# A hybrid encoder layer on one core: scan decays from sums sent as rows through DRAM, and the down-projection's weight sums formed one stage earlier

## The chip, the cores and the metric

The kernel runs on one core of a Trainium2 chip. The metric is device microseconds of one execution, the median of the runs shown. Engines are named as in the profile: PE is TensorE (PEld its weight loads), DVE VectorE, ACT ScalarE, POOL GpSimd, SP SyncE, whose instruction stream issues all DMAs here. All data is fp32; products are made from values split into a rounded high part and a rest (`fp32r`), three matmuls for one product (`mm3`: L113, L114, L115).

## The reference

One encoder layer over a prompt of 2048 tokens and a sample of 256 tokens, width 1024: RMSNorm, an input projection, a latent attention group (8 heads) beside a Mamba-2 group (forward and backward scan over chunks of 128 tokens), an output projection, then SwiGLU. What the change touches:

```python
def decay_matrix(a_cs):
    diff = a_cs[..., :, None] - a_cs[..., None, :]
    return jnp.exp(jnp.where(mask, diff, -jnp.inf))       # mask: lower triangle

def ssd_scan(x, dt, a, bmat, cmat):
    xdt = x * dt[..., None]
    a_cs = jnp.cumsum(dt * a, axis=-1)                    # in each chunk
    scores = jnp.einsum('bclhn,bcshn->bchls', cc, bc) * decay_matrix(a_cs)
    y_diag = jnp.einsum('bchls,bcshp->bclhp', scores, xdt)
    ...
def encoder_layer(x, ...):
    ...
    return x + (jax.nn.silu(h @ w_gate) * (h @ w_up)) @ w_down
```

## The kernel before

The 2304 tokens are 18 tiles of 128 (a tile is also a chunk of the scan). The program runs in six stages, one after the other on PE.

**A, projections** (0 to 329 us): q, k, v, z and the scan's dt from the normed input; q, k, v, z and the transposed input (`d_hT`) go to DRAM. The first block is the sample, the next ones are prompt.

**B, SSD** (329 to 745 us): blocks of two tiles. `project` multiplies the x/B/C weights into the next block (96 products of 256 columns a chunk, L113 to L115); the convolution follows on DVE (L469, 16 a chunk) with ACT beside it. `decays(c)` builds the decay matrix of a chunk for both directions: three masked copies on POOL (`rh`, `rl`, `dm`, L488), two matmuls for each half of the heads (L505, L506) that turn the masked step sizes into differences of sums, Exp on ACT (L507), the factor dt on DVE (L508), and the sum of both directions (L510). `turn(c)` transposes the chunk; `scan(c)` multiplies the decays into the scores (L538), forms states (L554, L557, L558) and outputs (L567, L568), and stores `d_y` and `d_sb`. A tile scheduler sets the order on each engine; pools give SBUF slots.

**C, attention** (745 to 1605 us): per head k, v and q are loaded (L654 to L666), scores, softmax and product follow in a written order.

**D, out-projection** (1605 to 1875 us), with the residual stored as `d_x2`.

**E, gate/up** (1883 to 2891 us): a fast (Strassen-like, 7 products for 2x2 blocks) matmul over three groups of six tiles; the operand `hB` is transposed from normed tiles `o` (L919, L932, L933), `U` holds its sums; the weight sums `ws` come from `rawf` loads. SwiGLU's outputs go to DRAM as `d_A`.

**F, down-projection** (2891 us to the end): the same scheme, 7 products by 9 operands by 33 matmuls of 512 columns = 2079 matmuls. `columns(m, j)` (L1114 to L1127) loads blocks of `w_down` (`rawd`), subtracts them on POOL (L1118, L1121, L1124), and splits them on ACT (L1126) and DVE (L1127) into 16 slots `wd`; `operand` loads and splits `d_A` (L1134, L1135).

Of the kernel before, what the change touches and what calls it, by code (L numbers as in the profile page):

```python
# [36 lines left out]
MAGIC = float(0x5F3759DF)  # L37


@with_exitstack  # L40
def hymba_kernel(ctx: ExitStack, tc: tile.TileContext, io, seqs, dbg=None):
# [50 lines left out]
    cmr = const.tile([P, 2, P], F32R, name="cmr")  # L92
    later.append(lambda: nc.vector.tensor_copy(cmr[:, 0, :], m_gt))
    later.append(lambda: nc.vector.tensor_copy(cmr[:, 1, :], m_lt))
# [8 lines left out]
    d_z, d_y, d_C, d_sb = ([dram.tile([P, SW if m != "C" else NG * P], F32, name=f"d_{m}{i}") for i in range(NT)] for m in ("z", "y", "C", "sb"))  # L103
    d_x2 = [dram.tile([P, D], F32, name=f"d_x2{i}") for i in range(NT)]
# [56 lines left out]
    with ExitStack() as ph:  # L161
# [4 lines left out]
        wa = wp.tile([P, 2, KD, WA], F32R, name="wa")  # L166
# [201 lines left out]
    dfs, dtd, dec, dts, dah, dal = (dpool.tile([P, 2, NT, SH], F32, name=m) for m in ("dfs", "dtd", "dec", "dts", "dah", "dal"))  # L368
    dsplit = dpool.tile([P, 2, NT, SH], F32, name="dsplit")

    with ExitStack() as ph:
# [5 lines left out]
        with ExitStack() as inner:  # L377
# [27 lines left out]
            dhr = sb.tile([P, 2, NT, SH], F32R, name="dhr")  # L405
# [3 lines left out]
            nc.vector.tensor_copy(dhr, dsplit)  # L409
            nc.vector.tensor_copy(dah, f(dhr))  # L410
            nc.vector.tensor_tensor(dal, dsplit, dah, op=ALU.subtract)
# [67 lines left out]

        def decays(c, even):  # L480

            w = []
            for d in range(2):
                sign = 1 - 2 * d

                def masked(dst, a):

                    nc.gpsimd.affine_select(dst, a[:, d, c, :].rearrange("p (h o) -> p h o", o=1).to_broadcast([P, SH, P]), pattern=[[0, SH], [sign, P]], compare_op=ALU.is_ge, fill=0.0, base=0, channel_multiplier=-sign)  # L488
# [22 lines left out]
            return w[0]  # L511

# [58 lines left out]
        def decay_sums():  # L571
            for d, (m1, m2) in enumerate(((m_le, m_gt), (m_ge, m_lt))):
# [4 lines left out]
                nc.vector.tensor_tensor(dtd[:, d], dtd[:, d], dts[:, d], op=ALU.mult)  # L577

# [3 lines left out]
        for b in range(nb + 2):  # L582
# [8 lines left out]
            for u in range(4):  # L591
# [21 lines left out]
    mpool = pool(mixer, "mla", 1, side="right")  # L613
# [161 lines left out]

    with ExitStack() as ph:
# [23 lines left out]
        def gather(c):  # L800
# [26 lines left out]
            junk = sb.tile([P, SW], F32, name="junk3", tag="junk3", bufs=1)  # L827
# [7 lines left out]
        def turned(c, y):  # L835
            mT = mp.tile([P, 2, KD, P], F32R, name="mT", tag="mT", bufs=3)
# [7 lines left out]
        def project(c, mT):  # L844
# [9 lines left out]
            if c in order[:4]:  # L854
# [392 lines left out]
```

## Time and profile before

| What | us |
| --- | --- |
| Median of three runs | 3412.65 (3410.53 to 3413.48) |
| The profiled execution | 3416.36 |
| Span of the profile | 3414.7 |
| PE busy | 3244.2 (95% of the span) |
| DVE busy | 2456.1 (72%) |
| ACT busy | 1698.0 (50%) |
| POOL busy | 609.4 (18%) |

A busy time counts instructions in flight; at a lower granted clock the same matmul counts longer. Waits name the instruction that came last before the waiting one could start. The rows of the trace stand in a section of their own below.

### The profile page before, as it was taken

What the parts mean: (1) busy time and instruction counts of PE and PEld (TensorE: products, weight loads), DVE (VectorE), ACT (ScalarE), POOL (GpSimd) and SP (SyncE); (2) the same over time, 40 slices, a digit from 0 to 9 for tenths busy, and PEclk for the clock granted to TensorE, in tenths of its full rate; (3) what the DMA queues carried; (4) which work ended last, traced back from release to release, by engine and by line L of the source; (5) the groups of instructions that cost most, each with busy time, mean ns of one, the idle gap of its engine ahead of it and who ended that gap; (6) DMA issues with size and microseconds to landing.
All of it is one profiled execution on the core that took longest, in us unless ns stands there. A gap on an engine that the chain in (4) does not pass through costs nothing.

```text
span 3414.7 us, 48534 instructions
## 1 busy us (share of the span) xinstructions
PE 3244.2 (95%) x17817; PEld 2882.8 (84%) x17817; DVE 2456.1 (72%) x4396; ACT 1698.0 (50%) x3518; POOL 609.4 (18%) x597
## 2 busy tenths in 40 slices
PE   8998999879999999999799799999999999999988
PEld 7897988858888888887688699999999998778777
DVE  6445799978888888887854777787778776354566
ACT  5453444437777777777311545455544444222233
POOL 2222577750000000000310000000000000432630
PEclk9999999979999999999899899999999999999999
DMA  6565222231022111200642333333333333755664
GB/s 253 191 227 186 90 81 75 69 83 37 27 54 52 39 40 41 54 17 15 224 139 99 142 115 122 142 118 118 137 141 132 113 119 118 230 185 172 224 212 137
DMA packets 259166, 407.24 MB, mean 119 GB/s; under 512 B 21424, under 2 KB 170608, under 8 KB 256368
## 3 DMA queue, kind: packets, MB, share of 16 engines
q1 hardware_dynamic: 258928, 404.15, 35.5%
q8 instruction: 140, 2.29, 0.3%
q14 instruction: 98, 0.80, 0.1%
HBM read 274.98 MB, written 129.11 MB: 118 GB/s over the span
## 4 chain that ended last, share of the span: by engine, by line
PE 78%; DVE 11%; DMA 3%; POOL 3%; issue 3%; ACT 2%; SPq 0%; POOLq 0%; ACTq 0%; DVEq 0%
PE bank_mb L1005 8%; PE bank_ma L1005 8%; PE bank_ta L1005 8%; PE bank_ma L113 6%; PE bank_ma L115 6%; PE bank_ma L114 6%; PE bank_mb L113 5%; PE bank_mb L115 5%; PE bank_mb L114 5%; DVE Y L469 4%; PE bank_ta L721 4%; PE bank_o L729 3%; PE bank_o L730 3%; DMA rawd<-w_down 2%; PE bank_tb L721 2%
## 5 line engine op out<-in xcount | busy, mean ns | idle before, releaser
L938 DVE TENSOR_TENSOR ws<-rawf,ws 128x512 fp32r<-128x512 f32 x396 | 267.8, 687 | 97.2 <-ACT ws L937 95.3
L937 ACT ACTIVATE ws<-rawf 128x512 fp32r<-128x512 f32 x396 | 241.8, 627 | 171.7 <-PE bank_ta L1005 37.2
L1005 PE MATMUL bank_ma<-U,ws 128*128 128x384 f32 x1584 | 302.8, 338 | 6.4 <-ACT U L937 3.2
L1005 PE MATMUL bank_mb<-U,ws 128*128 128x384 f32 x1584 | 304.2, 336 | 2.8 <-ACT c L1014 2.5
L1005 PE MATMUL bank_ta<-U,ws 128*128 128x384 f32 x1584 | 297.3, 334 | 3.5 <-ACT U L937 3.0
L1005 PEld LDWEIGHTS bank_ma<-U,ws 128*128 128x128 f32 x1584 | 279.0, 190 | 8.0 <-ACT U L937 3.5
L129 DVE TENSOR_TENSOR pT<-bank_ta,pT 128x512 fp32r<-128x512 f32 (+1 forms) x352 | 239.6, 681 | 63.2 <-ACT pT L128 54.6
L1005 PEld LDWEIGHTS bank_mb<-U,ws 128*128 128x128 f32 x1584 | 277.4, 189 | 5.1 <-ACT c L1014 4.1
L1005 PEld LDWEIGHTS bank_ta<-U,ws 128*128 128x128 f32 x1584 | 276.7, 188 | 4.5 <-ACT U L937 3.3
L128 ACT ACTIVATE pT<-bank_ta 128x512 fp32r<-128x512 f32 (+1 forms) x352 | 209.1, 595 | 116.7 <-PE bank_ta L721 116.2
L1118 POOL TENSOR_TENSOR rawd<-rawd 128x512 f32<-128x512 f32 x33 | 51.5, 1559 | 1189.0 <-DMA rawd<-w_down 1188.6
L729 PE MATMUL bank_o<-pT,v 128*128 128x512 f32 x528 | 248.7, 471 | 1.9 <-ACT ot L736 1.9
L469 DVE SCALAR_TENSOR_TENSOR Y<-X,cw,Y 128x256 f32<-128x256 f32 x288 | 218.5, 815 | 22.9 <-POOL X L456 15.4
L679 DVE TENSOR_REDUCE mx<-bank_ma 128x1 f32<-128x512 f32 (+1 forms) x261 | 177.0, 678 | 50.1 <-PE bank_ma L115 49.5
L721 PE MATMUL bank_ta<-ident,pr 128*128 128x128 f32 x1388 | 210.6, 273 | 2.0 <-DVE pT L129 2.0
L721 PEld LDWEIGHTS bank_ta<-ident,pr 128*128 128x128 f32 x1388 | 170.5, 140 | 48.7 <-DVE pT L129 8.0
L730 PE MATMUL bank_o<-pT,v 128*128 128x512 f32 x528 | 206.2, 391 | 0.0
L1134 ACT ACTIVATE as<-rawa 128x1408 fp32r<-128x1408 f32 x63 | 86.7, 1378 | 225.6 <-PE bank_ma L115 108.6
L688 ACT ACTIVATE pr<-bank_mb,mx 128x512 f32<-128x512 f32 (+1 forms) x261 | 181.4, 695 | 7.9 <-DVE mx L679 4.8
L688 ACT ACTIVATE pr<-bank_ma,mx 128x512 f32<-128x512 f32 (+1 forms) x261 | 179.1, 686 | 6.4 <-DVE mx L707 5.5
L679 DVE TENSOR_REDUCE mx<-bank_mb 128x1 f32<-128x512 f32 (+1 forms) x261 | 176.9, 678 | 7.0 <-PE bank_mb L115 3.7
L752 POOL TENSOR_TENSOR mla<-lo,ri 128x256 f32<-128x256 f32 (+1 forms) x40 | 22.8, 570 | 855.6 <-DVE lo L751 842.5
(399 smaller groups left out, 8584.9 us busy)
## 6 DMA issues: line engine op xcount, KB each, us to landing
rawf<-w_gu SPq DMA_DIRECT2D x66, 1024.0 KB, 5.8
rawa<-d_A SPq DMA_DIRECT2D x63, 704.0 KB, 5.2
rawd<-w_down SPq DMA_DIRECT2D x154, 256.0 KB, 4.9
d_A<-c SPq DMA_DIRECT2D x132, 192.0 KB, 1.9
d_A<-s SPq DMA_DIRECT2D x99, 192.0 KB, 1.9
o<-d_x SPq DMA_DIRECT2D x32, 512.0 KB, 4.8
d_hT<-hT SPq DMA_DIRECT2D x7, 2048.0 KB, 12.9
hT<-d_hT SPq DMA_DIRECT2D x7, 2048.0 KB, 7.9
```

The costliest lines, as they stand in the source:

```text
L113: nc.tensor.matmul(ps, wh, xh, start=start, stop=False)
L114: nc.tensor.matmul(ps, wh, xl, start=False, stop=False)
L115: nc.tensor.matmul(ps, wl, xh, start=False, stop=stop)
L469: nc.vector.scalar_tensor_tensor(y[:, j, :], x[:, j, t:t + n], cw[:, j, t:t + 1], y[:, j, :], op0=ALU.mult, op1=ALU.add)
L679: nc.vector.tensor_reduce(mx[:, j:j + 1], ps[:, :m * P], axis=AX.X, op=ALU.max, negate=nch == 1)
L688: nc.scalar.activation(e[:, :m * P], ps[:, :m * P], AF.Exp, bias=bias, accum_out=rs[:, i, j:j + 1])
L721: nc.tensor.transpose(ps[:, i * P:(i + 1) * P], pr[i, kt // 4][:, kt % 4 * P:(kt % 4 + 1) * P], ident)
L729: nc.tensor.matmul(po[0][:, :n], v[:, s0 + kt, :], pT[:, 0, :n], start=kt == 0, stop=False)
L730: nc.tensor.matmul(po[0][:, :n], v[:, s0 + kt, :], pT[:, 1, :n], start=False, stop=kt == sn - 1)
L937: nc.scalar.activation(dst[:, 0], src, AF.Copy)
L938: nc.vector.tensor_tensor(dst[:, 1], src, f(dst)[:, 0], op=ALU.subtract)
L1005: nc.tensor.matmul(ps[:, :W], w[:, a, k, :], x[:, b, k, :], start=k + n == 0 and not more, stop=k == HK - 1 and n == 2, skip_group_check=more)
```

## The change

It has five parts.

1. **Decays as rows.** Sums over a chunk are formed once (`decay_sums`: a coarse and a fine part of the steps, each multiplied by the triangle, and ln dt less the fine sum), transposed and stored to DRAM by `cum_rows` (`d_cum`, `d_off`). For each chunk `load_rows` brings them back by 14 small DMAs (6 of 32 KB, 8 of 4 KB) into `rows0/1` and `offs0/1`; `decays` multiplies these, adds a large negative mask by a second matmul (`never`, `identr`), and Exp gives decay times dt. The masked copies (L488) and the factor dt (L508) go. `d_cum` has to be zero off its diagonal: one DMA of 3.98 MB copies zeros into it at the start. The conv's edge copies (L455, L456) go from POOL to ACT.
2. **Sums of weight blocks in gate/up.** In the third group of stage E, `sums(j)` loads two row blocks of `w_down`, makes four subtractions on POOL and stores the results as `d_B`; stage F loads these, so the subtractions in `columns` go.
3. **Early columns and operands in F.** Five columns of the next product and one operand are prepared ahead; `as` takes the slots of `hB`; the residual's addition (L1176) goes from POOL to DVE.
4. **The first gate/up operand in D.** `columns_of(0, 0)` transposes the first three tiles inside the out-projection; the pools of E stand in another order.
5. **Alignment.** `wa` is padded from 432 to 448 columns, `f_pad` shifts `wd`, and the attention's pool `mla` goes to the other side of SBUF.

```diff
+            if b == 1:
+                nc.sync.dma_start(d_cum.rearrange("q g x -> (q g) x"), io["c_zero"])
...
-                rh = mp.tile([P, SH, P], F32R, name="rh", tag="rh")
-                rl = sb.tile([P, SH, P], F32R, name="rl", tag="rl", bufs=1)
-                dm = sb.tile([P, SH, P], F32, name="dm", tag="dm", bufs=1)
-                masked(rh, dah)
-                masked(rl, dal)
-                masked(dm, dts)
+                r, o = fix[d]
...
-                    nc.tensor.matmul(pd, cmr[:, d, :], rh[:, s, :], start=True, stop=False)
-                    nc.tensor.matmul(pd, cmr[:, d, :], rl[:, s, :], start=False, stop=True)
+                    nc.tensor.matmul(pd, o, r[:, s, :], start=True, stop=False)
+                    nc.tensor.matmul(pd, identr, never[:, d:d + 1, :].to_broadcast([P, 4, P]), start=False, stop=True)
                     nc.scalar.activation(e[:, s, :], pd, AF.Exp)
-                nc.vector.tensor_tensor(e, e, dm, op=ALU.mult)
...
+        def load_rows(c):
+            for d in range(2):
+                r, o = fix[d]
+                for q in range(3):
+                    at = (0, 8, 32)[q]
+                    nc.sync.dma_start(f(r)[at:at + SH], d_cum[q, d * NT + c, :SH * SH * P].rearrange("(h x l) -> h x l", h=SH, l=P))
+                for q in range(4):
+                    at = (16, 24, 40, 48)[q]
+                    nc.sync.dma_start(f(o)[at:at + SH], d_off[q, d * NT + c])
...
+        def cum_rows():
+
+            d_diag = d_cum.rearrange("q (t r) (h x) -> q (r h) t x", t=3, h=SH)[..., :P]
+            for src, qc, qo in ((coarse, (0, 1), (0, 1)), (fine, (2,), ()), (off, (), (2, 3))):
...
                     decay[c] = decays(c, b % 2 == 0)
+                    if c + 1 < NT:
+                        load_rows(c + 1)
...
-    mpool = pool(mixer, "mla", 1, side="right")
+    mpool = pool(mixer, "mla", 1)
...
+            if c == order[G]:
+                columns_of(0, 0, [first_xs.pop(t) for t in order[:G]])
...
+        def sums(j):
+
+            top, low = (op.tile([P, D], F32, name="o", tag="o") for _ in range(2))
+            nc.gpsimd.tensor_copy(top[:, :1], C["c11", 0][:, :1])
+            nc.sync.dma_start(top, io["w_down"][j])
+            nc.sync.dma_start(low, io["w_down"][j + HF])
+            b11, b12, b21, b22 = top[:, :512], top[:, 512:], low[:, :512], low[:, 512:]
+            for m, out, x, y in ((5, b11, b12, b11), (7, b12, b22, b12), (6, b22, b22, b11), (4, b21, b21, b22)):
+                nc.gpsimd.tensor_tensor(out, x, y, op=ALU.subtract)
+                nc.sync.dma_start(d_B[m][:, j], out)
...
-        rp = pool(ph, "f_raw", 6)
+        rp = pool(ph, "f_raw", 4)
...
+                nc.sync.dma_start(raw, d_B[m][:, j])
...
+        prepare(1, AHEAD)
+        ahead = operand(*work[0])
+        for i, (m, s, t) in enumerate(work):
+            lo, hi = parts[s]
+            prepare(m, HF)
+            a = ahead
+            if i + 1 < len(work):
+                ahead = operand(*work[i + 1])
+            if i % n_m == n_m - 2 and i + 2 < len(work):
+                prepare(work[i + 2][0], AHEAD)
```

**SP at the start of stage A**, before: `cs` is a table, `xt` the input, `raw` the weights of z, kv and q, `d_hT` a store.

```order
L207 DMA cs<-c_rope 128x32 x2
L184 DMA xt<-x 128x1024 x4
L207 DMA cs<-c_rope 128x32
L174 DMA raw<-w_z 128x1024 x3
L174 DMA raw<-w_kv 128x1024
L174 DMA raw<-w_q 128x2x384 x2
L338 DMA d_hT_84<-hT 128x4096
```

Now:

```order
L209 DMA cs<-c_rope 128x32 x2
L186 DMA xt<-x 128x1024 x4
L209 DMA cs<-c_rope 128x32
L329 DMA d_cum<-c_zero 64x15552
L176 DMA raw<-w_z 128x1024 x3
L176 DMA raw<-w_kv 128x1024
L176 DMA raw<-w_q 128x2x384
L342 DMA d_hT_83<-hT 128x4096
```

The copy of zeros `d_cum<-c_zero` stands ahead of the three loads of z's weights and all that follows them.

**SP in the scan's loop**, before: `hT` is the next block's input, `d_C`, `d_y` and `d_sb` are the chunks' stores.

```order
L427 DMA hT<-d_hT_84 128x4096
L569 DMA d_y_126<-yo 128x512
L473 DMA d_C_145<-Y 256x1x128
L473 DMA d_C_146<-Y 256x1x128
L564 DMA d_sb_162<-ns_6111 128x512
L569 DMA d_y_127<-yo 128x512
L564 DMA d_sb_163<-ns_6345 128x512
```

Now (`rows`, `offs`: what `load_rows` brings):

```order
L433 DMA hT<-d_hT_83 128x4096
L508 DMA rows_3521<-d_cum 8x1024 x3
L511 DMA offs_3522<-d_off 8x128 x2
L608 DMA d_y_125<-yo 128x512
L511 DMA offs_3522<-d_off 8x128 x2
L479 DMA d_C_144<-Y 256x1x128
L479 DMA d_C_145<-Y 256x1x128
L508 DMA rows_3527<-d_cum 8x1024 x3
L511 DMA offs_3528<-d_off 8x128 x4
L603 DMA d_sb_161<-ns_6185 128x512
L508 DMA rows_3521<-d_cum 8x1024 x2
L608 DMA d_y_126<-yo 128x512
```

Fourteen loads a chunk now stand between the stores, those of one direction in a row.

**SP at the end of the scan**, before: `k` and `v` are those of attention's first head.

```order
L564 DMA d_sb_165<-ns_6789 128x512
L654 DMA k<-d_k_93 64x4608
L655 DMA k<-d_kr 32x4608
L657 DMA v<-d_v 128x18x128
L569 DMA d_y_130<-yo 128x512
L564 DMA d_sb_166<-ns_6999 128x512
L473 DMA d_C_151<-Y 256x1x128
L473 DMA d_C_152<-Y 256x1x128
```

Now:

```order
L603 DMA d_sb_166<-ns_7156 128x512
L608 DMA d_y_131<-yo 128x512
L608 DMA d_y_132<-yo 128x512
L603 DMA d_sb_167<-ns_7239 128x512
L603 DMA d_sb_168<-ns_7301 128x512
L608 DMA d_y_133<-yo 128x512
L603 DMA d_sb_169<-ns_7351 128x512
L702 DMA k<-d_k_92 64x4608
L703 DMA k<-d_kr 32x4608
```

The first head's `k` and `v` were issued among the stores of the chunks, five chunks ahead of the last; they now stand behind the last `d_sb`.

## Rows read from the trace of the kernel before

**Rows 1.** Busy time by stage; columns: stretch, its length, engines, granted clock, DMA

```profile
329.00:745.00 416.00, 362.58 (x2467) 335.17 (x2468) 364.03 (x414) 168.26 (x264) 292.51 (x268) 0.92 0.22 75
745.00:1605.00 860.00, 847.71 (x4759) 691.79 (x4759) 705.86 (x1276) 662.09 (x1647) 21.18 (x37) 0.99 0.16 41
...
1900.00:2891.00 991.00, 979.25 (x5638) 972.66 (x5638) 748.20 (x1355) 475.42 (x889) 0.00 (x0) 0.99 0.34 122
```

**Rows 2.** The same view: the scan's loop and its tail

```profile
345.00:685.00 340.00, 309.64 (x2232) 292.04 (x2231) 301.68 (x352) 146.64 (x231) 239.80 (x226) 0.96 0.24 81
685.00:745.00 60.00, 41.68 (x170) 32.99 (x169) 48.63 (x51) 15.09 (x23) 41.77 (x30) 0.72 0.12 43
```

**Rows 3.** Groups of VectorE, 329 to 745 us; columns: busy, mean, idle and releaser

```profile
L469 DVE SCALAR_TENSOR_TENSOR Y<-X,cw,Y 128x256 f32<-128x256 f32 x288 | 218.5, 815 | 22.9 <-POOL X L456 15.4 <-ACT Y L467 7.2
L508 DVE TENSOR_TENSOR e<-e,dm 128x1024 f32<-128x1024 f32 x36 | 60.9, 1691 | 14.5 <-ACT e L507 6.5 <-POOL dm L488 4.3 <-POOL rh L488 3.7
```

**Rows 4.** The convolution's line L469 by itself

```profile
L469 DVE SCALAR_TENSOR_TENSOR Y<-X,cw,Y x288: 468/476/1511, 334.4 to 710.4; 128x256 f32<-128x256 f32 x144
```

**Rows 5.** Groups of GpSimd, 329 to 745 us

```profile
L488 POOL TENSOR_SCALAR_AFFINE_SELECT rh<-dah 128x1024 fp32r<-128x1024 f32 x36 | 52.9, 1470 | 38.7 <-PE bank_ta L505 38.7
L488 POOL TENSOR_SCALAR_AFFINE_SELECT rl<-dal 128x1024 fp32r<-128x1024 f32 x36 | 51.3, 1424 | 0.0
...
L488 POOL TENSOR_SCALAR_AFFINE_SELECT dm<-dts 128x1024 f32<-128x1024 f32 x36 | 47.5, 1320 | 31.4 <-DVE e L508 31.4
```

**Rows 6.** Waits of TensorE, whole span; columns: total us, times, longest us

```profile
PE bank_o L567 <- DVE e L538: 23.3, 12, 3.5
PE bank_tb L554 <- DVE ns L558: 21.3, 9, 5.9
...
PE bank_ma L113 <- ACT as L1134: 10.0, 3, 6.6
...
PE bank_mb L113 <- ACT wd L1126: 7.4, 3, 4.6
```

**Rows 7.** Timeline of SyncE around the scan's end; columns: start, length

```profile
671.53 0.52 SPq L654 DMA_DIRECT2D k<-d_k  x1
...
747.30 0.32 SPq L564 DMA_DIRECT2D d_sb<-ns  x1
```

**Rows 8.** DMA issues: KB each, median us from issue to landing

```profile
d_hT<-hT SPq DMA_DIRECT2D x7, 2048.0 KB, 12.9
hT<-d_hT SPq DMA_DIRECT2D x7, 2048.0 KB, 7.9
...
k<-d_k SPq DMA_DIRECT2D x8, 1152.0 KB, 9.3
...
d_y<-yo SPq DMA_DIRECT2D x18, 256.0 KB, 2.0
```

**Rows 9.** Timeline of SyncE at the start

```profile
16.64 2.56 SPq L174 DMA_DIRECT2D raw<-w_z  x3
```

**Rows 10.** Timeline of TensorE, out-projection to gate/up

```profile
1874.55 0.39 PE L115 MATMUL bank_mb<-wo,mT 128*128 128x512 f32 x1
...
1883.45 1.01 PE L1005 MATMUL bank_ma<-U,ws 128*128 128x384 f32 x2 [1.76 <-ACT ws L937]
...
1899.98 0.48 PE L932 MATMUL bank_tb<-ident,o 128*128 128x128 f32 x1 [9.15 <-DVE o L919]
```

**Rows 11.** Busy time in three stretches of the down-projection

```profile
2891.00:2997.00 106.00, 91.97 (x378) 73.70 (x377) 48.23 (x45) 36.95 (x48) 44.71 (x29) 0.92 0.77 238
3100.00:3200.00 100.00, 100.00 (x442) 82.81 (x442) 53.31 (x56) 29.44 (x33) 29.52 (x14) 1.00 0.59 183
3220.00:3300.00 80.00, 65.51 (x259) 50.95 (x258) 45.02 (x63) 20.73 (x26) 57.14 (x30) 0.91 0.75 241
```

**Rows 12.** Groups of the down-projection

```profile
L1118 POOL TENSOR_TENSOR rawd<-rawd 128x512 f32<-128x512 f32 x33 | 51.5, 1559 | 1189.0 <-DMA rawd<-w_down 1188.6
L1126 ACT ACTIVATE wd<-rawd 128x512 fp32r<-128x512 f32 x76 | 44.3, 623 | 98.9 <-POOL rawd L1124 57.6 <-POOL rawd L1121 19.3 <-POOL rawd L1114 11.3
```

More of the change, by code (lines that the diff above doesn't have):

```diff
@@ L367, in hymba_kernel @@
     dpool = pool(mixer, "decays", 1)
-    dfs, dtd, dec, dts, dah, dal = (dpool.tile([P, 2, NT, SH], F32, name=m) for m in ("dfs", "dtd", "dec", "dts", "dah", "dal"))
+    dfs, dtd, dec, dts, coarse, fine, off = (dpool.tile([P, 2, NT, SH], F32, name=m) for m in ("dfs", "dtd", "dec", "dts", "coarse", "fine", "off"))
     dsplit = dpool.tile([P, 2, NT, SH], F32, name="dsplit")
@@ L511, in decays @@
             return w[0]
+        def cum_rows():
+            d_diag = d_cum.rearrange("q (t r) (h x) -> q (r h) t x", t=3, h=SH)[..., :P]
+            for src, qc, qo in ((coarse, (0, 1), (0, 1)), (fine, (2,), ()), (off, (), (2, 3))):
+                flat = src.rearrange("p d c h -> p (d c h)")
+                ps = bank("mb")[:96, :384]
+                for t in range(3):
+                    nc.tensor.transpose(ps[:, t * P:(t + 1) * P], flat[:, t * 96:(t + 1) * 96], ident)
+                part = sb.tile([96, 2, 3, P], F32R, name="part", tag="Y")
+                flatp = part.rearrange("p q t l -> p q (t l)")
+                nc.scalar.activation(flatp[:, 0], ps, AF.Copy)
+                if src is not fine:
+                    nc.vector.tensor_tensor(flatp[:, 1], ps, f(flatp)[:, 0], op=ALU.subtract)
+                for i, q in enumerate(qc):
+                    nc.sync.dma_start(d_diag[q], f(part)[:, i])
+                for i, q in enumerate(qo):
+                    nc.sync.dma_start(d_off[q].rearrange("(t r) h l -> (r h) t l", t=3), f(part)[:, i])
         def turn(c, y):
@@ L577, in decay_sums @@
                 nc.vector.tensor_tensor(dtd[:, d], dtd[:, d], dts[:, d], op=ALU.mult)
+                for t in (coarse, fine):
+                    ps = bank("mb")[:, :NT * SH]
+                    nc.tensor.matmul(ps, m1, t[:, d].rearrange("p c h -> p (c h)"), start=True, stop=True)
+                    nc.vector.tensor_copy(t[:, d], ps.rearrange("p (c h) -> p c h", h=SH))
+                nc.vector.tensor_tensor(off[:, d], off[:, d], fine[:, d], op=ALU.subtract)
+            cum_rows()
+            load_rows(bl[0][0])
         nb = len(bl)
@@ L773, in hymba_kernel, with columns_of @@
                 step()
+    G = 3
+    W = G * P
+    assert NT % (2 * G) == 0
+    order = [c for c, _ in falling(1)]
+    parts = [(order[i:i + G], order[i + G:i + 2 * G]) for i in range(0, NT, 2 * G)]
+    hbs = [pool(ctx, "e_hb0", 1, side="right")]
+    H, first_xs = {}, {}
+    def columns_of(s, half, xs):
+        h = hbs[half].tile([P, KD, W], F32, name=f"hB{half}", tag="hB")
+        for k in range(KD):
+            ps = bank(("tb", "o")[k % 2])
+            for i in range(G):
+                nc.tensor.transpose(ps[:, i * P:(i + 1) * P], xs[i][:, k * P:(k + 1) * P], ident)
+            nc.scalar.activation(h[:, k, :], ps[:, :W], AF.Copy, scale=g_ffn[:, k:k + 1])
+        H[s, half] = h
     with ExitStack() as ph:
@@ L1081, in hymba_kernel @@
                 weights(*groups[i + AHEAD])
+            if s + 1 == len(parts) and u and m == 1:
+                sums(j)
             if s + 1 < len(parts) and u:
@@ L1224, in layout @@
     ang = np.arange(s, dtype=np.float32)[:, None] * inv[None, :]
+    rk = np.zeros((P, P + SH * P), np.float32)
+    rk[:16, :P] = rk[32:40, :P] = 1.0
+    for q, at in enumerate((16, 24, 40, 48)):
+        rk[at:at + SH, P:] = np.repeat(np.eye(SH), P, axis=1) * (1.0 if q > 1 else -1.0)
+    out["c_rk"] = rk
+    out["c_zero"] = np.zeros((6 * (a["x_prompt"].shape[1] + a["x_sample"].shape[1]) // P, SH * (SH + 1) * P), np.float32)
     out["c_rope"] = np.stack([np.cos(ang), np.sin(ang)], axis=1).astype(np.float32)
```

171 lines of the change are left out of this document (81 added, 90 removed).

## The prediction

> **What bounds the kernel now.** I read the busy times by stage first, then cut the stages whose sum is short of their length, then the waits, then the groups and the timelines at those places. PE is busy for 3244.2 of 3414.7 us, so at most 170 us are idle; but a matmul counts longer at a low clock, so the idle hides more. Attention and gate/up leave little: 847.7 of 860 and 979.3 of 991 us, at a clock of 0.99 [rows 1]. The SSD stage leaves most: 362.6 of 416, with DVE at 364.0, POOL at 292.5 [rows 1]. Inside it there are two regimes. In the loop PE is busy for 309.6 of 340 us at a clock of 0.96, DVE for 301.7; in the tail, where no projection is left to fill gaps, PE for 41.7 of 60 at 0.72 [rows 2]. PE's two longest waits of the whole program lie here, L567 for e of L538 (23.3 us) and L554 for ns of L558 (21.3 us), both for DVE [rows 6]. DVE is slow there for a reason: L469 takes 476 ns as a median and 815 as a mean [rows 3, 4], the rest being stretch while POOL runs its masked copies [rows 5]. The second place is the down-projection. 442 matmuls fill 100 us undisturbed, so one takes 0.2262; but 378 take 106 us at its start, 259 take 80 us at 3220 [rows 11]. Those stretches wait for operands and columns (L1134, L1126) [rows 6], and the columns wait for POOL [rows 12]. The third is the seam into gate/up: the last out-projection matmul starts at 1874.55, the first product at 1883.45, and a transpose at 1899.98 has waited for 9.15 us [rows 10].
>
> **The change part by part.** The sum is made against the profiled execution, 3416.36 us, which lies 3.7 above the median.
>
> *Zeros at the start.* One copy of 3.98 MB goes ahead of z's weights, issued at 16.64 now [rows 9]. The nearest rows: a load of 2 MB lands after 7.9 us, a store of 2 MB after 12.9 as a median [rows 8]. So the copy holds the queue for 16 (two loads) to 26 us (two stores), or for as little as 10 if it moves at twice the load's rate. The order of PE is changed too: z's matmuls of the sample stand behind other work. I take +5, with 0 and +15 as ends, since the queue may also let the weights overtake. The Trainium skill, "DMA: Bandwidth & Descriptors", section "Latency and other measured facts", gives 207 to 214 GB/s for copies between HBM tensors; from this an estimate of 19 us for the copy, inside these ends, and no row here shows such a copy.
>
> *The scan's loop.* Gone from POOL are three groups of 36 copies, 52.9 + 51.3 + 47.5 = 151.7 us [rows 5], and small edge copies; some 115 of 292.5 us stay. Gone from DVE are 36 products L508, 60.9 us [rows 3]. L469's stretch is 288 x (0.815 - 0.476) = 97.6 us [rows 3, 4]; if it scales with POOL's time, 115/292.5, 38 us of it are left, so 59 more go. DVE falls from 364 to about 364 - 61 - 59 = 244 us, a third less. Added are no PE instructions: two matmuls of 512 columns take the place of two. Then PE sets the pace: 309.6 us at a clock of 0.96 are 297 at full clock, and with some 8 us of gaps left the loop takes 305 instead of 340, **-35**; I take -32, with -15 (only half of the waits of rows 6 go) and -43 (no gap at all) as ends. This term rests on the row loads being hidden. They are 14 a chunk, and a chunk takes 340/18 = 19 us or more; DMAs of 256 KB land after 2.0 us [rows 8], and issues follow each other by 0.5 us (0.52 for k) [rows 7], so 14 x 0.5 + 2 = 9 us if they overlap. Behind them in SP's order stand the stores d_y, d_sb, d_C and the load of hT, none of which PE needs within a chunk. If a load of hT (7.9 us) is in front, 17 us: still hidden, though barely.
>
> The rule that speaks against this: in the Trainium skill, the page "DMA: Bandwidth & Descriptors", section "Rules for kernel authors", says that many small transfers should be made one, since under 64 KB one pays mostly overhead. All 14 are under 64 KB. By the rule the overhead is paid on the queue, and as long as it is under a chunk's time the sum stays; where it isn't is the third rival.
>
> *The scan's start.* Sums, nine transposes, seven stores to DRAM and the first 14 loads stand in a chain ahead of the first decays: 2.0 for a store, 2.0 + 7 for the loads, an estimated 3 for three copies of about an ACT group's length [rows 12] between, 12 to 14 us; beside it the first blocks' projections run, and the waits for rh go. +3, with -2 and +10 as ends.
>
> *The tail.* 60 us, in which DVE is busy for 48.6 [rows 2]. By the same third, 32 us of DVE; PE needs 41.7 x 0.72 = 30 us at full clock. The chain through both is serial in part: a third off its 60 us gives 40, and 3 more for loads that a shorter chunk covers less: 43, **-17**, ends -8 and -24. What is late next is the rows: here chunks follow faster than in the loop, and 9 us of loads stand in each.
>
> *Attention's first loads.* The first head's k is issued at 671.53, 74 us ahead of the last d_sb at 747.30 [rows 7], and lands long before it is wanted. In the changed order it stands behind the last d_sb. A k load takes 9.3 us [rows 8], v behind it a little longer; PE has nothing else to do, and goes cold. **+11**, ends +5 (short because the tail's last work covers some) and +15.
>
> *Attention and alignment.* The matmul counts don't change. Addresses do, in attention and in the down-projection. 512 columns at 2.4 GHz are 213.3 ns, an undisturbed one takes 226.2 [rows 11]; no row shows the same matmul at another address, so what of the 12.9 ns between is due to the address is unknown. I take 0, the value for an address without effect, with a loss or a gain as ends; rival (4) has the gain's price.
>
> *The seam into gate/up.* From 1874.55 to the transpose at 1899.98 are 25 us, in which 9.15 + some 5 us PE idles and the clock is low [rows 10]. The first operand is now ready in D; its U sums still wait for DVE and ACT. **-10**, ends -4 and -15. The transposes are moved, not removed.
>
> *Sums in gate/up.* 44 subtractions of 1.56 us [rows 12] are 69 us of POOL in the last third, 330 us, where POOL does nothing now; at L469's price, 97.6/292.5 = 0.33 us of DVE for one of POOL, that is 23 us on a DVE that is busy for 748 of 991 [rows 1]. Hidden by DVE's room; and 66 DMAs more, behind which the rawf loads stand on SP. +2, ends 0 and +8.
>
> *The down-projection.* The two disturbed stretches lose 106 - 378 x 0.2262 = 20.5 and 80 - 259 x 0.2262 = 21.4 us [rows 11], together 42. POOL leaves the columns' path, five columns and one operand are there early, each column is one load instead of up to four. What remains is some 6 us at the stage's start. **-36**, ends -22 and -42.
>
> Sum: 5 - 32 + 3 - 17 + 11 + 0 - 10 + 2 - 36 = **-74**: 3416.4 - 74 = 3342 profiled, 3339 as a median.
>
> **The rivals.**
> (1) *Half of the scan.* The waits for DVE go, and waits for rows or for the chain ns to L554 come, so that the loop gives -15 and the tail -8: 26 us less, 3365. For it: the scan's state is a chain through PE, POOL (L557) and DVE, which the change doesn't shorten. Against: most waits of rows 6 name DVE while it is full.
> (2) *The down-projection keeps half.* Five early columns of eleven are not enough, or four rawd buffers instead of six bind, 3357 to 3360; with (1) 3383.
> (3) *Slower: the rows bind.* If the 14 loads went one behind the other, each landing before the next, they would take 14 x 2.0 = 28 us a chunk [rows 8], and 18 chunks 504 us, 160 more than the forecast has: 3500. The change is slower than before from 74/18 = 4.1 us a chunk beyond 19, that is from 1.65 us for a load. For it: one queue, in order, and tiles with one buffer each, so a chunk's rows can't come before the last chunk's are read. Against: three loads of z's weights, each twice the 256 KB that take 2.0 us [rows 8], are issued within 2.56 us [rows 9], so one doesn't wait for the landing of the last.
> (4) *Alignment counts.* If the shifted operands save all of the 12.9 ns in each of the down-projection's 2079 matmuls, that is 27 us: 3312, and lower if attention's do too. The rows speak neither for it nor against it; by the same token a matmul could become slower.
> (5) *The zeros stall PE.* If z's weights wait for the whole copy at the store's rate and PE finds nothing else, that is 26 us instead of 5: 3360.
>
> **How the numbers follow.** Forecast (3325 to 3355) 0.50; (1) 0.15; (2) 0.08; (4) 0.09; (5) 0.08; (3) 0.07; gains and costs that cancel to no difference 0.03. The likeliest is 3339. The range goes from 3300, which takes in (4) with a few us of attention's, to 3390, which takes in (5), (1), (2) and (2) with (1); what is out is (3), no difference, and the far end of (4): about 0.14. Under 0.2% (6.8 us) can't be told from no change; faster by more 0.90, within 0.03, slower 0.07.
>
> **What would show it.** In the scan: L469's mean near 0.6 us, L508 gone, PE's loop at 300 to 310 us with a clock near 1; a wait of the L505 matmuls for DMA rows would show (1) or (3). After the last d_sb, PE waiting for some 10 us for a DMA of k. At 17 to 50 us, PE waiting for z's weights for under 15 us. In the down-projection, 2079 matmuls in 476 to 482 us and no wait for wd of more than 3 us; rows of rawd waiting for a buffer would show (2). The forecast is wrong if the loop stays over 325 us, or if the copy of zeros stalls PE for 20.

## The result, and the profile after

The changed kernel takes 3352.47 us as a median (3351.20 to 3356.65, four runs) against 3411.86 of before (3410.53 to 3413.48): the ratio is 0.9825, with a 95% interval of 0.9814 to 0.9837, or 59 us faster. The forecast was 3339, its range 3300 to 3390. The profiled execution has a span of 3350.0 us against 3414.7, 64.7 less.

The stages are cut here at the starts of the same matmuls in the two traces, and each term of the prediction stands beside its stretch. The second row holds the prediction's loop and the scan's start before it. Attention's first product is that of the softmax with v (L729 before, L777 after); the first scores, k with q, come ahead of it. The first block of gate/up is its first 168 matmuls.

| Stretch | Before | After | Change | Predicted |
| --- | --- | --- | --- | --- |
| Start to the first scan projection | 305.8 | 308.8 | +3.0 | +5 (zeros) |
| First to last scan projection | 371.2 | 327.3 | -43.9 | -32 and +3 |
| To the last L593 (L554 before) | 69.0 | 52.5 | -16.5 | -17 |
| To attention's first product | 25.9 | 41.4 | +15.5 | +11 |
| Attention and out-projection | 1102.7 | 1102.2 | -0.5 | 0 |
| Seam and first block of gate/up | 68.6 | 48.1 | -20.5 | -10 |
| Rest of the first two groups | 626.6 | 626.6 | 0.0 | |
| Third group of gate/up | 321.2 | 344.3 | +23.1 | +2 |
| Down-projection | 514.1 | 489.3 | -24.8 | -36 |
| End | 9.6 | 9.5 | -0.1 | |

The sum, -64.7, is 9 short of the forecast -74, but four terms are off by ten or more, two each way. The busy times of the scan after (columns as in [rows 2]), first the loop, then the tail:

```profile
348.00:636.00 288.00, 287.69 (x2195) 278.15 (x2195) 208.59 (x323) 146.88 (x276) 84.98 (x79) 1.00 0.28 97
636.00:689.00 53.00, 41.20 (x204) 32.90 (x202) 35.70 (x52) 21.30 (x36) 25.49 (x19) 0.86 0.22 71
```

PE has no gap left in the loop, 287.69 of 288 us at a clock of 1.00, where [rows 2] show 0.96; DVE has come down to 209 us of 288. DVE's convolution there:

```profile
L475 DVE SCALAR_TENSOR_TENSOR Y<-X,cw,Y 128x256 f32<-128x256 f32 x288 | 172.4, 660 | 31.8 <-ACT X L462 30.9 <-ACT Y L473 0.9
```

```profile
L475 DVE SCALAR_TENSOR_TENSOR Y<-X,cw,Y x288: 464/476/1518, 348.3 to 664.0; 128x256 f32<-128x256 f32 x144
```

The mean fell from 815 to 660 ns, the median is 476 as in [rows 4]. TensorE's waits after, of the whole span:

```profile
PE bank_ta L1071 <- DVE c L1085: 13.9, 9, 4.0
PE bank_ma L115 <- DMA k<-d_kr: 12.9, 1, 12.9
...
PE bank_ma L115 <- ACT as L1194: 4.6, 1, 4.6
PE bank_tb L593 <- DVE ns L597: 4.2, 2, 3.3
...
PE bank_o L606 <- DVE e L577: 3.1, 2, 2.5
```

The 23.3 and 21.3 us of [rows 6] for the scan are now 3.1 for e and 4.2 for ns. Two waits are new: 12.9 us for the first head's k and 13.9 us in nine pieces for DVE's L1085 in gate/up. The timeline of SP shows where the first comes from, and that of PE where it ends:

```profile
689.88 0.32 SPq L603 DMA_DIRECT2D d_sb<-ns  x1
690.30 0.52 SPq L702 DMA_DIRECT2D k<-d_k  x1
```

```profile
687.45 1.72 PE L593 MATMUL bank_tb<-xd,bt 128*128 128x256 f32 x4 [0.95 <-DVE ns L597]
702.10 0.77 PE L115 MATMUL bank_ma<-k,q 96*128 96x512 f32 x1 [12.93 <-DMA k<-d_kr]
702.67 0.63 PE L116 MATMUL bank_ma<-k,q 96*128 96x512 f32 x1
703.09 0.63 PE L117 MATMUL bank_ma<-k,q 96*128 96x512 f32 x1
```

The load of k stands right behind the last `d_sb`, as the order said, and the first score starts 12 us later; the matmuls behind it follow each other at 0.42 us, where [rows 11] have 0.226 at full clock. Before, k was issued at 671.53 [rows 7], and 18 of the first head's score matmuls ran inside the scan's tail, from 683.95 on; now all of them come behind it. The zeros show at the start on POOL, which splits z's weights. Before, and then after:

```profile
24.54 1.06 POOL L119 TENSOR_SCALAR wz<-raw 128x1024 fp32r<-128x1024 f32 x1 [10.15 <-DMA raw<-w_z]
```

```profile
38.19 3.04 POOL L121 TENSOR_SCALAR wz<-raw 128x1024 fp32r<-128x1024 f32 x2 [5.42 <-DMA raw<-w_z]
```

The weights come 13.7 us later on POOL, but PE, with z's products moved behind other work, loses 3.0 of them. The DMA records of the trace show the copy itself: its 64 rows of 62,208 bytes move between 21.0 and 33.5 us, that is 3.98 MB in 12.4 us, and end 16.7 us after the issue at 16.76.

### The profile page after: what moved, and what is told of

Its sections match the earlier page's. It is cut to its first block, busy times and chain, and to the rows that moved or that the text cites. A ratio compares the mean times of both kernels' runs of the same rounds, so it can differ in the third digit from the quotient of the medians.

```text
span 3350.0 us, 48726 instructions
## 1 busy us (share of the span) xinstructions
PE 3220.2 (96%) x17834; PEld 2869.8 (86%) x17834; DVE 2347.6 (70%) x4390; ACT 1703.3 (51%) x3576; POOL 344.9 (10%) x393
## 4 chain that ended last, share of the span: by engine, by line
PE 80%; DVE 8%; DMA 6%; ACT 2%; issue 2%; POOL 2%; SPq 0%; ACTq 0%; DVEq 0%; POOLq 0%
PE bank_ma L115 8%; PE bank_ma L117 8%; PE bank_ma L116 8%; PE bank_ma L1071 6%; PE bank_mb L1071 6%; PE bank_ta L1071 6%; PE bank_mb L115 6%; PE bank_mb L117 6%; PE bank_mb L116 6%; PE bank_ta L769 4%; PE bank_o L777 3%; PE bank_o L778 3%; PE bank_tb L769 2%; DMA rawf<-w_gu 1%; DVE ws L1004 1%
## 5 line engine op out<-in xcount | busy, mean ns | idle before, releaser
L1004 DVE TENSOR_TENSOR ws<-rawf,ws 128x512 fp32r<-128x512 f32 x396 | 278.6, 717 | 68.8 <-ACT ws L1003 67.6
L1071 PE MATMUL bank_ta<-U,ws 128*128 128x384 f32 x1584 | 301.6, 337 | 21.2 <-DVE c L1085 13.9
L777 PE MATMUL bank_o<-pT,v 128*128 128x512 f32 x528 | 249.7, 473 | 1.9 <-ACT ot L784 1.9
L475 DVE SCALAR_TENSOR_TENSOR Y<-X,cw,Y 128x256 f32<-128x256 f32 x288 | 172.4, 660 | 31.8 <-ACT X L462 30.9
L736 ACT ACTIVATE pr<-bank_ma,mx 128x512 f32<-128x512 f32 (+1 forms) x261 | 179.1, 686 | 20.5 <-DVE mx L755 19.4
L117 PE MATMUL bank_ma<-hT,wx 128*128 128x256 f32 x576 | 164.7, 286 | 2.7 <-DVE wx L126 2.7
L115 PE MATMUL bank_ma<-hT,wx 128*128 128x256 f32 x576 | 166.9, 290 | 0.3 <-ACT wx L123 0.3
```

What stands on the lines that cost most here:

```text
L115: nc.tensor.matmul(ps, wh, xh, start=start, stop=False)
L117: nc.tensor.matmul(ps, wl, xh, start=False, stop=stop)
L736: nc.scalar.activation(e[:, :m * P], ps[:, :m * P], AF.Exp, bias=bias, accum_out=rs[:, i, j:j + 1])
L777: nc.tensor.matmul(po[0][:, :n], v[:, s0 + kt, :], pT[:, 0, :n], start=kt == 0, stop=False)
L1004: nc.vector.tensor_tensor(dst[:, 1], src, f(dst)[:, 0], op=ALU.subtract)
L1071: nc.tensor.matmul(ps[:, :W], w[:, a, k, :], x[:, b, k, :], start=k + n == 0 and not more, stop=k == HK - 1 and n == 2, skip_group_check=more)
```

## The experiments

A time without a range behind it is a single run. Stretches that the kernels leave alone differ a little among the traces: the third group of gate/up takes 342.3 to 347.1 us in six kernels that share it, the down-projection 488.3 to 491.9 in eight. A difference of that size shows nothing.

**The scan alone.** The kernel before with part 1 of the change and nothing else; attention's pool stays on the right side, so that k keeps its place. The line is shown against the changed kernel, and parts 2 to 5 are missing too.

```diff
-    mpool = pool(mixer, "mla", 1)
+    mpool = pool(mixer, "mla", 1, side="right")
```

> The kernel before with the decays as rows alone (zeros, sums, rows, the conv's edge copies on ACT), attention's pool where it was; here the first k keeps its place ahead of the last stores. Theory, from the two traces: start +3, loop -44, tail -16, and no wait for k: -57 or 3355. Rival: the 15 us at the seam are due to the rows' own end, not to k's slots: 3370.

Measured: 3355.11 us (3354.25 to 3356.35), ratio 0.9832 (0.9817 to 0.9846). The loop is 327.0, the tail 51.3 and the stretch to the first product 27.1 us, not 41.4. So the scan gives 58 us, and all the rest of the change together 2.6 (4.6 by the spans of the profiles), which the two intervals do not tell from nothing. That rest is made of gains and losses: against this kernel the seam gains 69.2 - 48.1 = 21.1 and the down-projection 510.7 - 489.3 = 21.4, and of these 42.5 go 41.4 - 27.1 = 14.3 to k and 344.3 - 321.2 = 23.1 to the weight sums.

**k early.**

```diff
+        kvs = [pool(ph, "c_kv0", 1)]
+        qp = pool(ph, "c_q", 2)
         lp = pool(ph, "c_l", 2)
-        qp = pool(ph, "c_q", 2)
-        kvs = [pool(ph, "c_kv0", 1)]
```

> The changed kernel with the attention's pools opened in another order (k and v of even heads first, then q, then the rest), so that the first head's k and v get the slots of the projection weights, which are free from 636 us on, and stand five chunks ahead of the last d_sb in SP's order. Theory: the wait of the first scores for k (12.9 us) and the cold stretch behind it are what the change pays at this seam, 15.0 us between the last L593 and the last out-projection matmul; the time falls by 13 to 16 us, to 3336 to 3340. Rival: the first scores can't do much before the first head's softmax has filled its pipeline, so the wait moves to the row maxima; the time falls by 3 at most, to 3349.

Measured: 3340.13 us (3338.37 to 3340.77), 12.3 under the changed kernel; the stretch to attention's first product is 27.0 us, as in the scan alone. PE behind the last L593:

```profile
690.02 0.50 PE L115 MATMUL bank_tb<-k,q 96*128 96x512 f32 x1 [0.74 <-ACT ns L599]
...
693.75 0.79 PE L115 MATMUL bank_ma<-k,q 96*128 96x512 f32 x1 [2.76 <-ACT pr L736]
```

The first scores run inside the scan's tail again (18 matmuls, from 649.6 us on), and the next ones follow the scan at once; 2.8 us of the rival's wait for the softmax are left. The theory's mechanism holds; its gain falls 0.7 us short of the range.

**The weight sums in attention.**

```diff
+                if nch > 1 and h > 1 and todo_sums:
+                    sums(todo_sums.popleft(), ri[:, 0, :])
...
-            if s + 1 == len(parts) and u and m == 1:
-                sums(j)
```

> The changed kernel with the weight-block sums (loads, four subtractions on POOL, stores) moved from the third group of gate/up into the attention, eleven times after a block of 512 rows. Theory: POOL's subtractions slow those DVE instructions that read both inputs from SBUF, and gate/up has them while attention's read one from PSUM; the third group goes from 344 back to 321 us, attention stays at 829, F's start gains 0 to 4: 3326 to 3331. Rival: DVE in attention (busy for 706 of 860 us) is slowed as much, and the gain comes back there: 3340 or more.

Measured: 3330.52 us (3329.47 to 3332.08), 22.0 under the changed kernel. The third group is 321.7 us; attention, from its first product to its last score, is 829.2 in both; the down-projection is 488.6: its start gained nothing. So the rival fell. DVE's groups in the third group show why the place matters. In the changed kernel, with POOL's subtractions beside them:

```profile
L1004 DVE TENSOR_TENSOR ws<-rawf,ws 128x512 fp32r<-128x512 f32 x126 | 95.7, 781 | 4.7 <-ACT ws L1003 4.7
L1089 DVE TENSOR_TENSOR c<-c,c 128x384 f32<-128x384 f32 x32 | 25.9, 810 | 1.0
L1085 DVE TENSOR_TENSOR c<-bank_ta,c 128x384 f32<-128x384 f32 x42 | 23.1, 550 | 4.6 <-PE bank_ta L1071 4.4
```

And with the sums in attention:

```profile
L1008 DVE TENSOR_TENSOR ws<-rawf,ws 128x512 fp32r<-128x512 f32 x137 | 92.2, 688 | 39.1 <-ACT ws L1007 38.8
L1089 DVE TENSOR_TENSOR c<-bank_ta,c 128x384 f32<-128x384 f32 x44 | 24.2, 551 | 2.1 <-ACT c L1084 1.2 <-PE bank_ta L1075 0.9
L1093 DVE TENSOR_TENSOR c<-c,c 128x384 f32<-128x384 f32 x34 | 18.8, 553 | 1.0
```

The split of `ws` is 781 ns against 688 and the sum `c<-c,c` 810 against 553, both with two inputs in SBUF; `c<-bank_ta,c`, with one of them in PSUM, is 550 against 551. The Trainium skill, "SBUF — State Buffer", says under "Who interferes with whom" that a VectorE instruction with two SBUF inputs contends with a GpSimd instruction that reads SBUF, and one with at most one SBUF input, outside the 2-port modes, does not; these three rows agree. In attention the largest group of DVE, with one input in PSUM (`pT<-bank_ta,pT`), takes 689 ns with the sums and without.

But it is not this stretch that PE waits for in most of the group. The changed kernel's trace shows another way, by the order of SP, here once in full:

```profile
2674.73 4.88 POOL L999 TENSOR_TENSOR o<-o 128x512 f32<-128x512 f32 x3 [0.95 <-DMA d_A<-c]
```

```profile
2679.64 0.32 SPq L1000 DMA_DIRECT2D d_B<-o  x1
2680.05 2.15 SPq L1039 DMA_DIRECT2D rawf<-w_gu  x2
```

```profile
2686.39 0.69 DVE L1049 TENSOR_TENSOR S<-rawf 128x512 f32<-128x512 f32 x1 [9.28 <-DMA rawf<-w_gu]
```

```profile
2689.41 2.38 PE L1071 MATMUL bank_ta<-U,ws 128*128 128x384 f32 x12 [2.20 <-DVE c L1085]
```

A store of `d_B` waits until POOL has made its block; the load of the next weights, `rawf`, is issued behind it; DVE sits idle for 9.28 us until that load lands, and L1085, for which PE waits, comes 2.4 us later. Eight of the nine waits for L1085 come 3.0 us after the end of such a wait of DVE, 10.0 us in all; the ninth, 3.95, stands at the group's end, behind DVE's split of the early operand (`as`). DVE's waits for `rawf` in the third group, in the changed kernel and then with the sums in attention:

```profile
DVE S L1049 <- DMA rawf<-w_gu: 69.1, 10, 9.3
```

```profile
DVE S L1053 <- DMA rawf<-w_gu: 28.3, 10, 3.2
```

Only at the group's start does PE wait beside stretched instructions with no such load in front: 4.3 us for DVE's `U`, while POOL makes its first four blocks.

**The traffic without the subtractions.**

```diff
-                nc.gpsimd.tensor_tensor(out, x, y, op=ALU.subtract)
```

> The changed kernel without the four subtractions on POOL in the third group of gate/up; the loads and the stores stay, so that raw blocks are stored as sums and the down-projection multiplies wrong weights (this part of the computation is left out). Theory (POOL's reads hold up DVE's instructions with two SBUF inputs): the third group goes from 344 to 321 to 324 us, the whole to about 3329. Rival (66 more DMAs and stores in SP's order hold the gate/up loads back): it stays at 338 or more, the whole at 3346 or more.

Measured: 3332.63 us; the third group takes 324.9. So POOL's subtractions cost 19.4 of the 23.1 us, and the 66 DMAs, with POOL's one-column copies that stay, 3.7, which is hardly more than the traces differ by. The theory's number holds, but the run does not tell its reason from the other: without the subtractions the stores don't wait for POOL either, and DVE's waits for `rawf` are 28.2 us.

**Shorter subtractions.**

```diff
-                nc.gpsimd.tensor_tensor(out, x, y, op=ALU.subtract)
+                for p in range(0, 512, 128):
+                    nc.gpsimd.tensor_tensor(out[:, p:p + 128], x[:, p:p + 128], y[:, p:p + 128], op=ALU.subtract)
```

> The changed kernel with each of the 44 subtractions cut into four of 128 columns. The same work on POOL in shorter instructions. Theory: DVE waits for the POOL instruction that is in flight, 1.56 us at most now and some 0.4 to 0.5 then, and PE waits only where a DVE instruction is late by more than its bank's slack; the third group falls to 325 to 333 us. Rival: what counts is POOL's time in sum, which grows with the fixed time of 132 more instructions; the third group stays at 344 or rises to 350.

Measured: 3365.27 us, the third group 358.3, slower by 14. POOL's group in the changed kernel, then in this one, and this one's largest wait of PE there, a group of DVE and SP's waits for POOL:

```profile
L999 POOL TENSOR_TENSOR o<-o 128x512 f32<-128x512 f32 x44 | 70.6, 1604 | 56.8 <-DMA o<-w_down 51.1 <-DMA d_A<-c 3.8
```

```profile
L1000 POOL TENSOR_TENSOR o<-o 128x128 f32<-128x128 f32 x176 | 105.4, 637 | 47.9 <-DMA o<-w_down 47.9
```

```profile
PE bank_ta L1072 <- DVE c L1086: 21.8, 11, 4.1
```

```profile
L1090 DVE TENSOR_TENSOR c<-c,c 128x384 f32<-128x384 f32 x32 | 18.9, 590 | 1.0
```

```profile
SPq L1001 <- POOL o L1000: 80.6, 44, 3.7
```

The theory, that the single wait matters, fell; the group even rose above the rival's 350. POOL's time rose from 70.6 to 105.4 us, and less the 3.7 of the DMAs PE lost 19.4 and 33.4: 0.27 and 0.32 us for each us of POOL. DVE is stretched less (`c<-c,c` 590 ns instead of 810; DVE is busy for 243 us of the group instead of 255, and for 235 without the subtractions), and PE loses more. So the stretch is not what PE pays for. SP's waits for POOL fit: 80.6 us instead of 56.0, and with them DVE's waits for `rawf`, 85.4 instead of 69.1. No run changes SP's order alone.

**The subtractions on DVE.**

```diff
-                nc.gpsimd.tensor_tensor(out, x, y, op=ALU.subtract)
+                nc.vector.tensor_tensor(out, x, y, op=ALU.subtract)
```

> The changed kernel with the 44 subtractions on DVE instead of POOL. DVE gets 44 x 0.69 = 30 us more in a stretch of 330 us where it is busy for 241, and POOL is idle. Theory: no instruction is stretched, the third group is 321 to 325 us, the whole 3329 to 3333. Rival: DVE's queue is in order, a subtraction waits for its load, and what stands behind it waits too: 335 or more.

Measured: 3345.16 us (3343.36 to 3347.32), the third group 337.0: 7 less than on POOL, 12 more than with the traffic alone, 15 more than with the sums in attention. The subtractions in DVE's queue, and PE's waits:

```profile
L999 DVE TENSOR_TENSOR o<-o 128x512 f32<-128x512 f32 x44 | 30.2, 686 | 25.8 <-DMA o<-w_down 25.5
```

```profile
PE bank_ta L1071 <- DVE c L1085: 6.7, 2, 6.4
PE bank_ta L1071 <- DVE ws L1004: 4.1, 4, 1.5
```

The theory's first half holds: with POOL idle the splits of `ws` and the sums `c<-c,c` take 682 and 549 ns, so no instruction is stretched. The subtractions take 0.69 us each, 30.2 in all, as expected, but DVE sits idle for 25.5 us until their loads land, SP waits for DVE's blocks for 46.4 us, and PE waits for DVE for 10.8. The rival's time holds; how the 12 us part between DVE's queue and SP's, no run shows.

**Without the alignment.**

```diff
-        wa = wp.tile([P, 2, KD, 448], F32R, name="wa")[..., :WA]
+        wa = wp.tile([P, 2, KD, WA], F32R, name="wa")
...
-        pool(ph, "f_pad", 1).tile([P, 16], F32, name="pad")
```

> The changed kernel with the first weights' rows of 432 columns and without the 64-byte pad in the down-projection. Theory: the pitch of a matmul does not depend on these addresses (0.2262 us in both traces): within 3 us of the changed kernel, 3349 to 3355. Rival: the pad saves up to 12.9 ns in each of 2079 matmuls: up to 27 us slower, 3379.

Measured: 3360.09 us (3359.33 to 3362.15), slower than the changed kernel by 7.6, outside the theory's 3 us. The down-projection takes 496.7 instead of 489.3; stage A, with `wa`, 308.8 as before. 100 us of undisturbed matmuls (columns as in [rows 11]) after, then without the pad:

```profile
3220.00:3320.00 100.00, 100.00 (x443) 82.81 (x442) 75.60 (x203) 36.72 (x49) 0.00 (x0) 1.00 0.56 183
```

```profile
3220.00:3320.00 100.00, 100.00 (x430) 80.56 (x429) 73.68 (x193) 37.70 (x50) 0.00 (x0) 1.00 0.55 180
```

443 matmuls and 430, that is 0.2257 and 0.2326 us. At this pitch 2079 matmuls are 14 us longer; PE also waits less for operands and columns in the slower kernel (7.5 us instead of 10.1), and 7.4 us are left. In the compiled programs the blocks of `w_down` (`wd`) then start 160 bytes past a multiple of 256 and the other operand (`as`) 224; in the kernel before both start at 160 and in the changed one both at 224, so the pad keeps a pitch that was there, and gains none.

**Another pad.**

```diff
-        pool(ph, "f_pad", 1).tile([P, 16], F32, name="pad")
+        pool(ph, "f_pad", 1).tile([P, 48], F32, name="pad")
```

> The changed kernel with a pad of 192 bytes instead of 64 ahead of the weights of the down-projection, so that they start at 96 beyond a multiple of 256 (224 now, 160 without a pad) where the other operand starts at 224. In both traces 100 undisturbed us hold 443 matmuls where the two starts agree; without the pad 430. Theory: the remainder by 128 is what has to agree: 443 again, the whole within 3 us of 3352. Rival: the remainder by 256: 430, 3359 or more.

Measured: 3362.57 us, the down-projection 497.3.

```profile
3220.00:3320.00 100.00, 100.00 (x432) 81.09 (x431) 72.91 (x191) 36.39 (x48) 0.00 (x0) 1.00 0.57 184
```

432 matmuls in 100 us: a remainder that agrees by 128 does not help here. The rival holds, for these two operands and four pairs of starts, that of the kernel before among them; why, no run shows. It is no rule for every matmul: in attention of the changed kernel, k starts at 224 for even heads and at 160 for odd ones, with q at 224, and the scores start some 0.232 us apart in both, where the down-projection's matmuls start 0.227 apart in the changed kernel and 0.233 without the pad.

**POOL busy in the scan.**

```diff
+                sign = 1 - 2 * d
+                for _ in range(2):
+                    nc.gpsimd.affine_select(e, e, pattern=[[0, SH], [sign, P]], compare_op=ALU.is_ge, fill=0.0, base=0, channel_multiplier=-sign)
                 w.append(e)
```

> The changed kernel with POOL kept busy in the scan: two masks in place on each decay matrix before the sum of both directions (72 instructions of about 1.4 us, some 100 us; they set to zero what is zero already). Theory: DVE is stretched again (the convolution's line from 0.66 us to 0.75 to 0.85 in the mean) but stays under PE's pace, so that the loop (325 us with full PE) is 325 to 333 us and only the tail pays, 52 to 58: the whole 3352 to 3366. Rival: PE needs DVE's results at once, and the loop gives back in proportion, two thirds of the masks' 152 us having cost 44: 340 us or more, the whole over 3370.

Measured: 3395.84 us. The loop is 355.5 (327.3), the tail 64.0 (52.5): most of the scan's gain is gone. The same stretch as above, the waits that came back, and the masks:

```profile
348.00:636.00 288.00, 276.37 (x2026) 264.67 (x2025) 215.26 (x300) 137.09 (x263) 135.86 (x128) 0.96 0.27 93
```

```profile
PE bank_o L609 <- DVE e L580: 15.7, 8, 3.4
PE bank_tb L596 <- DVE ns L600: 6.9, 3, 3.2
```

```profile
L532 POOL TENSOR_SCALAR_AFFINE_SELECT e<-e 128x1024 f32<-128x1024 f32 x72 | 83.1, 1156 | 82.8 <-ACT e L529 77.9 <-DMA rows<-d_cum 2.8
```

The theory fell. The convolution's mean is 753 ns, as expected, and DVE is busy for 215 of 288 us, hardly more than the 209 of the changed kernel; yet PE waits for it as in [rows 6] and gets 2026 matmuls done there instead of 2195: 83 us of POOL cost 40. A share of busy time under PE's pace is not enough. Which part of that is POOL's reads beside DVE's, and which the masks' place in the chain (they stand between Exp and the sum, and DVE sits idle for 39.6 us until one is done), this run does not part; nor does any run part POOL's copies from the factor dt that the change took off DVE.

**Without the early columns.**

```diff
-            if i % n_m == n_m - 2 and i + 2 < len(work):
-                prepare(work[i + 2][0], AHEAD)
```

> The changed kernel without the five early columns of each next product in the down-projection (the first product's and the operand one ahead stay). Theory: the weight sums formed earlier give most of the 25 us that the down-projection gained, since POOL was what the columns waited for; without the early columns each of the six product changes costs 1 to 2 us more: 489 us become 495 to 501. Rival: the early columns are what gained it: 510 us or more.

Measured: 3355.35 us, the down-projection 490.7 against 489.3. The 6 to 12 us of the theory did not come, nor did the rival's 20: 1.4 us lie within what the down-projection differs by among kernels that share it, so no gain of the early columns is shown. How the 25 us are divided between the sums formed earlier, the operand one ahead and the rest of part 3 stays open.

**Both edits together.** k early and the sums in attention.

> Both edits together. Theory: they lie in different stages and add, 36 to 42 us off the changed kernel: 3311 to 3317. Rival: the sums' loads in attention's DMA queue hold k and q back: 3325.

Measured: 3320.15 us (3316.69 to 3321.89), 32.3 under the changed kernel where the two alone give 12.3 and 22.0. The third group is 321.4 and the stretch to the first product 27.0; neither gives anything back. The sum is 2 us short of the two, and 3 outside the theory's range; the runs differ by 5.

**And six raw buffers.**

```diff
-        rp = pool(ph, "f_raw", 4)
+        rp = pool(ph, "f_raw", 6)
```

> The kernel with both edits (k early, sums in attention) and six raw buffers in the down-projection instead of four. 489 us there are 18 more than 2079 undisturbed matmuls need. Theory: the fifth and sixth column of the first product and those at one later product change wait for a buffer; with six, 4 to 8 us less, 3312 to 3316. Rival: their loads stand behind the stores of d_A and the loads of d_x2 in SP's order, and buffers change nothing: 3318 to 3322.

Measured: 3306.51 us (3306.01 to 3307.90), ratio to before 0.9691 (0.9675 to 0.9707); 13.6 under the kernel with both edits, more than the theory's 8; the two spans of the profiles are 10.7 apart. The down-projection takes 479.7 instead of 489.1, so 9.4 us are its own. PE's waits there with four buffers, then with six:

```profile
PE bank_ma L115 <- ACT as L1196: 4.5, 1, 4.5
PE bank_mb L117 <- DVE as L1197: 2.5, 1, 2.5
PE bank_ma L117 <- DVE as L1197: 2.0, 3, 0.9
PE bank_ma L116 <- DVE wd L1186: 1.1, 1, 1.1
PE bank_mb L115 <- ACT as L1196: 0.2, 1, 0.2
```

```profile
PE bank_ma L115 <- ACT as L1196: 2.9, 1, 2.9
PE bank_ma L116 <- DVE wd L1186: 2.2, 1, 2.2
PE bank_ma L117 <- DVE as L1197: 0.9, 1, 0.9
```

The waits fall from 10.3 to 6.0 us, and the time at the lower granted clock (1.2 GHz) from 10.2 to 3.4. The waits name the operand (`as`), and ACT's rows at a product change show how a column's load is behind one of them. With four buffers:

```profile
3042.21 1.31 ACT L1185 ACTIVATE wd<-rawd 128x512 fp32r<-128x512 f32 x2 [4.92 <-DMA rawd<-w_down]
3043.42 2.63 ACT L1196 ACTIVATE as<-rawa 128x1408 fp32r<-128x1408 f32 x2
```

And with six:

```profile
3033.27 1.39 ACT L1196 ACTIVATE as<-rawa 128x1408 fp32r<-128x1408 f32 x1 [0.67 <-PE bank_mb L117]
```

With four, ACT sits idle for 4.92 us until a column has landed, and the split of the operand stands behind it; with six, the columns are split by then and the operand waits for PE alone. So the theory's reason holds, and the rival fell. This kernel, 106 us under the one before and 46 under the changed one, is the best of the study.

## Why the prediction was right, and where its steps were not

The time lies in the range and the direction is right, but the nearness of the sum is in part luck: two terms gained 25 us more than forecast, and two came out 32 us worse.

- *Zeros*: +5 predicted, +3.0 measured. From the Trainium skill, "DMA: Bandwidth & Descriptors", section "Latency and other measured facts", the prediction had worked out an estimate of 19 us for the copy; the trace shows 12.4 us of moving, and 16.7 from issue to end. z's weights came 13.7 us later, which PE does not pay in full, since its order had moved.
- *The loop*: right in mechanism, mis-sized. With its start -29 was predicted, -43.9 came, the far end of the term. The 8 us of gaps that the prediction left did not remain. The row loads were hidden as costed: no wait of the matmuls for rows is among the listed ones, so rival (3) is out. The Trainium skill, "DMA: Bandwidth & Descriptors", section "Rules for kernel authors", says that under 64 KB one pays mostly overhead; PE saw none of it, busy for 287.69 of 288 us.
- *The reason given for it* was too narrow. The prediction reasoned from DVE's busy time; the run with POOL busy again shows PE waiting at nearly the same busy time of DVE, which there is late because it waits for POOL. And the stretch did not scale with POOL's time: 288 x (0.660 - 0.476) = 53 us are left where 38 were expected.
- *The tail*: -17, measured -16.5. Rival (1) did not come. The 18 scores that left the tail are not the reason: the scan alone keeps them there and has a tail of 51.3.
- *Attention's loads*: +11 was the load alone; +15.5 came, 12.9 for the wait and the rest with the 18 scores that had run inside the tail; PE is at the lower granted clock (1.2 GHz) for 23.1 us of this stretch, 12.7 before. The run with k early gives 14.4 us of this stretch back.
- *The seam*: -10 predicted, -20.5 measured, below its end of -15: the first product follows the last out-projection matmul after 0.8 us instead of 8.9, and the other 12.4 us were won behind it, where the 9.15 us wait of [rows 10] stood and matmuls ran at the lower clock.
- *Sums in gate/up*: the failed step. The term priced the way by SP ("66 DMAs more, behind which the rawf loads stand on SP") at +2, and counted the DMAs alone. It left out that the stores among them wait for POOL, and the `rawf` loads with them: SP waited for POOL's blocks for 56.0 us, DVE for `rawf` for 69.1 us instead of 28.3, and PE lost 23.1, 19.4 of it to the subtractions. DVE's stretch, priced at 23 and set at nothing, came as 20 us of DVE and was hidden but for 4.3 us at the group's start. Ends of 0 to +8 did not hold the sum.
- *The down-projection*: -36 predicted, -24.8 measured. What failed in it is that the columns would no longer hold PE up. Rival (2) is what happened in part: four raw buffers bound. With six, and both other edits, the gain is 34.4.
- *Alignment*: rival (4) did not come, but for a reason that the prediction did not have. The pitch in the down-projection does depend on the starts; before, they agreed already.

## What to carry to other kernels

Before work is put on an idle engine, follow its results: a store that waits for them holds up every load behind it on SP, and the engines that wait for these loads. Here the same work cost 23 us in gate/up and nothing in attention. An engine's busy share under PE's pace does not say that its results come in time. When a change moves several seams, cut both traces at the same matmuls and compare stretch by stretch: a total near the forecast can hide terms of 20 us of either sign. When SBUF slots are laid out anew, look at what the next stage's first loads now lie on.

## What the runs showed of the hardware that was not expected

- A 512-column fp32r matmul of the down-projection took 0.2257 us where its two operands start at the same remainder by 256 bytes, and 0.2315 to 0.2326 at the two pairs tried where they do not. Attention's scores started some 0.232 us apart either way.
- Cutting POOL instructions of 512 columns in four made them cost 105.4 us instead of 70.6, while DVE's sums with two inputs in SBUF beside them took 590 ns instead of 810.
- Four DMAs of 4 KB and three of 32 KB for each direction of a chunk, 14 in all, left PE busy for 287.69 of 288 us.
